# Mixer B's pair products on one stationary operand, compressed values in eight row tiles, and w_out prepared a tile earlier in a hybrid decoder layer

## The chip, the cores and the metric

The kernel runs on one core of one Trainium2 chip. The metric is the device time of one execution in microseconds (us), as the median of several runs; a profiled execution gives the trace. TensorE multiplies, VectorE (DVE) and ScalarE (ACT) do the elementwise work, GpSimd (POOL) a little, and SyncE (SP) issues the transfers. The trace shows TensorE's weight loads as an engine of their own, PEld, beside its matmuls, PE.

## The reference, cut to what matters

One decoder layer on 512 tokens of width 1024. Two mixers read one input projection, are gated, merged and put through one output projection, and a layer norm with a residual ends it.

```python
def layer(x):
    h = x @ w_in + b_in                       # 1024 -> 5912 columns
    o_a = nsa_attention(...) * silu(z_a)      # 8 heads: compressed, selected, window branches
    o_b = hgrn2(q_b, f_b, i_b, lb)            # 4 heads of 128 x 128 state
    o_b = rms_norm(o_b) * norm_g * silu(z_b)
    y = sigmoid(gm_a) * (o_a @ w_branch_a) + sigmoid(gm_b) * (o_b @ w_branch_b)
    return layer_norm(alpha * x + y @ w_out, ln_g, ln_b)

# the compressed branch: 31 blocks, per head a softmax over them
pc = masked_softmax(q @ kc.T * scale, cmp_end <= t)
o_cmp = pc @ vc                               # vc: 31 x 64 for each of two groups of four heads

# mixer B, in chunks of 64 tokens: b is the running sum of log-forget-gates within a chunk
qe = qf * exp(b); ke = k * exp(-b)
attn = where(causal, qe @ ke.T, 0)            # 64 x 64 for each chunk
o = attn @ v + qe @ state                     # and the state is carried from chunk to chunk
```

## The kernel before

Everything is laid out with channels on the 128 partitions and the 512 tokens along the free axis. Projections keep full accuracy by splitting each operand into a rounded high part and the rest (`split2`: a cast on ScalarE at line 147, a subtraction on VectorE at line 148) and multiplying three of the four combinations, so that one 128-column tile of a projection is 24 matmuls of 512 columns (`proj`). Products that are not split are issued in full precision; the trace shows each as two TensorE instructions.

TensorE's instructions are kept in the order of the code, and so are the transfers on SP. The other engines' instructions are placed by a scheduler that runs over the finished program. What TensorE does between projection matmuls is set by `_Weave`: every stage beside the projections is a generator, `weave.tick()` is called every second of the eight steps of a projection (after six matmuls), and each generator says in how many ticks it wants to go on. The table `D` holds these numbers.

Stages that matter here. `hgrn(h)` is mixer B for one of four heads. It works on pairs of 64-token chunks, 128 tokens to a pair: `e1` is the key times a decay, `qeM` the query times its decay, `at` the masked products of a pair, and the pair products are issued at lines 403 to 408. `cmp_kv` makes compressed keys `kcB` and values `vcB`, `cmp_scores` and `cmp_probs` make the softmax over blocks, and `attn_values` (line 683) multiplies probabilities and compressed values into `asum` before it goes through the selected and window branches; `attn_scores` makes the scores of these in six units. Products of part of the array stand for 32 or 64 partitions of an operand or a result.

After the projections come eight tiles of branch weights (`BRANCH`, line 873), each two groups of 12 matmuls, merged on VectorE (lines 892 and 896) into `y`. The output projection needs w_out with its column mean taken out and split: `load_out` loads 128 rows, `minus_mean` sums them on ScalarE (line 859), and `split_out` writes high and low parts (lines 868 and 869). In the branch loop, tile n loads w_out's tile n and sums and splits tile n-2; the last two are split behind the loop. Then four token tiles of 48 matmuls each form the output (line 918), with the layer norm on VectorE and the stores.

Buffers: a pool `t2` of 67 tiles of 128x512, shown as `t` in the trace, and four PSUM pools of two banks each: `pa` (projections), `pss` (scores and small products), `pst` (transposes, and the first output tile), `pso` (accumulated results). `wraw`, `whi`, `wlo` are a weight tile as loaded and its two parts.

Of the kernel before, what the change touches and what calls it, by code (L numbers as in the profile page):

```python
# [18 lines left out]
P = 128  # L19
# [3 lines left out]
EPS = 1e-5  # L23

# [22 lines left out]
def _columns(name):  # L47

    c = np.arange(_COLS[name], _COLS[name] + 128)
    if name[0] == "q" and name[1] != "b" or name[:2] == "za":  # L50
# [17 lines left out]
         r0=5, p0=4, p1=11, p2=2, b0=1, a0=1, a1=1, a2=1, a3=1, a4=2, a5=1, s0=17, s2=0, s3=1)  # L68
# [27 lines left out]
def layer_kernel(ctx: ExitStack, tc: tile.TileContext, xT, xn, w0, wi, wf, wv, small, brow, consts,  # L96
# [145 lines left out]
    vcB = cst.tile([P, 4, 128], F32, name="vcB")  # L242
    G.memset(vcB, 0.0)
# [120 lines left out]
    def hgrn(h):  # L364
# [3 lines left out]
        bc, kc, qc = chunks(b), chunks(k), chunks(qs[h])  # L368
# [9 lines left out]
        yield D["h2"]  # L378
        A.activation(e2, e2, AF.Exp)
        A.activation(e1, e1, AF.Exp)  # L380
        A.activation(eb, b, AF.Exp)
        ke = T2(256)
        kev = ke.rearrange("p (t s) -> p t s", s=64)
        A.activation(kev, bc[:, :, 0], AF.Exp, scale=-1.0)
# [5 lines left out]
        qeM, qeo = T2(), T2(256)  # L390
        ebc, qmc = chunks(eb), chunks(qeM)
        qov = qeo.rearrange("p (t s) -> p t s", s=64)
# [3 lines left out]
        V.tensor_tensor(qmc[:, :, 1], qov, ebc[:, :, 0, 63:64].to_broadcast([P, 4, 64]), ALU.mult)  # L396
# [13 lines left out]
        for v in range(2):  # L410
            V.copy_predicated(chunks(at[0:64])[:, v:4:2, 0],
                              tri[0:64, 0:64].unsqueeze(1).to_broadcast([64, 2, 64]),
                              chunks(pst_[64 * v:64 * v + 64])[:, v:4:2, 0])
        V.copy_predicated(chunks(at)[:, :, 1], tri[:, 64:128].unsqueeze(1).to_broadcast([P, 4, 64]),
                          chunks(pst_)[:, :, 1])
# [23 lines left out]
        A.activation(sq, po, AF.Square)  # L439
        A.copy(o, po)  # L440
# [55 lines left out]
    mvs, ready, vcp = [None, None], set(), []  # L496

    def cmp_kv():
# [30 lines left out]
        for g in range(2):  # L529
            for m in range(4):  # L530
                r = 32 * (2 * (m % 2) + g)
                dst, src = vcB[r:r + 32, m, 64 * g:64 * g + 64], ps[r:r + 32, 64 + 64 * g:128 + 64 * g]
                if m % 2:
                    V.tensor_copy(dst, src)
                else:
                    A.copy(dst, src)
        ready.add("cmp")
        yield 2
        vcp.extend((T2(dt=F32R), T2(dt=F32R)))
        split2(vcB.rearrange("p m d -> p (m d)"), *vcp)  # L540
# [52 lines left out]
    def cmp_scores():  # L593
# [12 lines left out]
        ss = T2(), T2()  # L606
        s6 = [s.rearrange("p (i m g n) -> p g i m n", i=4, m=2, g=2) for s in ss]
        for g in range(2):
            ps = transpose4(sT[g])
            p4 = ps.rearrange("p (i c m n) -> p c i m n", i=4, c=2, m=2)  # L610
            for c in range(2):
                V.tensor_tensor(s6[c][:, g], p4[:, c], cmask.unsqueeze(2).to_broadcast([P, 4, 2, 32]), ALU.add)
            yield 1
        for c in range(2):
            weave.start(cmp_probs(c, ss[c]), 2 * c)

    def cmp_probs(c, s):
        s3 = s.rearrange("p (x n) -> p x n", n=32)
        mx = SM(16, "mx")
# [8 lines left out]
        for m in range(2):  # L628
            mxm = mx.rearrange("p (i m g) -> p i m g", i=4, m=2)[:, :, m]
            V.tensor_tensor(mxm, mxm, gv.rearrange("p i (g m) b -> p i g m b", g=2)[:, :, :, 2 * c + m, 0], ALU.mult)  # L630
# [3 lines left out]
        PTc[c] = T2(dt=F32R), T2(dt=F32R)  # L634
        split2(ps, *PTc[c])
# [47 lines left out]
    def attn_values():  # L683
# [3 lines left out]
        yield D["b0"]  # L687
        for m in range(4):
            po = PO()
            hi, lo = (t[:, 128 * m:128 * m + 128] for t in vcp)  # L690
            T.matmul(po, hi, PTc[m // 2][0], start=True, stop=False)
            T.matmul(po, hi, PTc[m // 2][1], start=False, stop=False)
            T.matmul(po, lo, PTc[m // 2][0], start=False, stop=True)
            A.copy(asum[:, m], po)
            yield 1
# [139 lines left out]
    gm = {}  # L835
    for i in range(8):
        for c in "ab":
            name = "g%s%d" % (c, i)
            ps, m = proj(name)
            gm[name] = T2()  # L840
            with tc.issue_after(exps[-1]):
                A.activation(gm[name], ps, AF.Tanh, bias=hbias[:, m:m + 1], scale=0.5)


    wo, woraw = [], {}
    lg, lbn = [T2(), T2()], [T2(), T2()]

    def load_out(kt):
        if kt < 8:
# [183 lines left out]
```

## Time and profile before

| | |
|---|---|
| median of 3 runs | 438.39 us (437.7 to 438.88) |
| the profiled execution, its own time | 437.94 us |
| its span, first to last instruction | 436.1 us |
| TensorE busy | 428.6 us, 98% |
| VectorE busy | 304.3 us, 70% |
| ScalarE busy | 245.2 us, 56% |
| mean granted TensorE clock | 0.996 of 2.4 GHz |
| memory traffic | 41.93 MB read, 2.10 MB written |

A page of the profile gives busy time by engine, the chain of work that ended last (followed back from the last instruction to what released it), and groups of equal instructions. The trace also answers with timelines: instructions of one engine in order, equal ones merged, with the idle time before a row and what ended it in brackets. Ends of matmuls are modelled and overlap the next one's start, so the distance between starts is what an instruction costs.

### The profile page before, as it was taken

To read this page: it belongs to the slowest core of one execution; us is meant where nothing else is said; L and a number is where in the kernel's file an instruction comes from. 1 tells how busy PE (TensorE), PEld (TensorE's weight loads), DVE (VectorE), ACT (ScalarE), POOL (GpSimd) and SP (SyncE) were. 2 spreads that over 40 slices of the span, in tenths; PEclk is the share of its full clock that TensorE was granted. 3 is DMA by queue.
4 is the path that set the end of the run, shared out by engine and by line. 5 is a ranking of instruction groups with operands and counts; after the bars stand their busy time and mean duration, and the time that the engine had idled before them with its cause. 6 is when DMAs were issued, how large, how long until landed. Compare 5 with 4: busy or idle time off the path is not lost.

```text
span 436.1 us, 6086 instructions
## 1 busy us (share of the span) xinstructions
PE 428.6 (98%) x2185; PEld 359.6 (82%) x2185; DVE 304.3 (70%) x629; ACT 245.2 (56%) x490; POOL 16.3 (4%) x27
## 2 busy tenths in 40 slices
PE   9999999999999999999999999999999999999994
PEld 8888888888898878888888888888888888877884
DVE  5915669986887577976665666578755768875395
ACT  4434624613447553768866666688864646569300
POOL 2000000000010220000000010001001100000000
PEclk9999999999999999999999999999999999999998
DMA  8995400352330554132112211111212462153022
GB/s 270 396 357 173 176 0 1 86 145 74 114 95 0 170 155 157 51 116 78 48 48 59 87 51 48 50 48 48 99 48 98 167 220 87 57 157 134 1 102 92
DMA packets 20879, 47.57 MB, mean 109 GB/s; under 512 B 2929, under 2 KB 4593, under 8 KB 20849
## 3 DMA queue, kind: packets, MB, share of 16 engines
q1 hardware_dynamic: 20560, 46.92, 32.1%
q8 instruction: 17, 0.28, 0.3%
q10 hardware_dynamic: 288, 0.26, 0.2%
q14 instruction: 14, 0.11, 0.1%
HBM read 41.93 MB, written 2.10 MB: 101 GB/s over the span
## 4 chain that ended last, share of the span: by engine, by line
PE 93%; DVE 5%; ACT 1%; issue 0%; DVEq 0%; ACTq 0%
PE pa L104 59%; PE pss L104 15%; PE pso L104 12%; PE pst L108 5%; PE pst L104 2%; DVE t L869 1%; DVE t L892 1%; DVE t L148 1%; ACT t L147 1%; DVE t L896 1%; DVE wlo L148 0%; DVE t L950 0%; DVEq L1029 0%; DVE sm_nm L861 0%; DVE sm_bst L938 0%
## 5 line engine op out<-in xcount | busy, mean ns | idle before, releaser
L104 PE MATMUL pa<-t,whi 128*128 128x512 f32 x640 | 201.6, 396 | 0.0
L104 PEld LDWEIGHTS pa<-t,whi 128*128 128x128 f32 x640 | 117.0, 188 | 24.5 <-issue 1.2
L104 PE MATMUL pa<-t,wlo 128*128 128x512 f32 x320 | 125.1, 391 | 0.0
L104 PEld LDWEIGHTS pa<-t,wlo 128*128 128x128 f32 x320 | 60.1, 188 | 13.1
L147 ACT CAST whi<-wraw 128x1024 fp32r<-128x1024 f32 x46 | 48.2, 1047 | 33.7 <-PE pa L104 20.1
L148 DVE TENSOR_TENSOR wlo<-wraw,whi 128x1024 fp32r<-128x1024 f32 x46 | 57.8, 1261 | 12.0 <-ACT whi L147 11.8
L664 DVE CUSTOM_DVE_ANT_0 t<-pss,t 128x512 f32<-128x512 f32 (+3 forms) x64 | 30.1, 488 | 24.0 <-PE pss L104 24.0
L148 DVE TENSOR_TENSOR t<-pst,t 128x512 fp32r<-128x512 f32 x42 | 28.9, 690 | 17.3 <-ACT t L147 17.2
L667 ACT ACTIVATE t<-t,sm_mn 128x512 f32<-128x512 f32 (+3 forms) x64 | 35.8, 560 | 9.1 <-DVE sm_mn L664 7.4
L104 PE MATMUL pso<-t,t 128*128 128x512 f32 (+2 forms) x170 | 36.9, 352 | 0.0
L104 PE MATMUL pa<-t,t 128*128 128x512 f32 (+1 forms) x168 | 36.7, 375 | 0.0
L104 PE MATMUL pss<-t,t 128*128 128x512 f32 (+4 forms) x238 | 36.1, 307 | 0.0
L147 ACT CAST t<-pst 128x512 fp32r<-128x512 f32 x42 | 24.3, 579 | 20.4 <-PE pst L108 20.3
L104 PEld LDWEIGHTS pa<-t,t 128*128 128x128 f32 x168 | 30.3, 188 | 5.6
L104 PEld LDWEIGHTS pss<-t,t 128*128 128x128 f32 (+1 forms) x238 | 29.3, 176 | 3.7 <-DMA wraw<-in_wf_dram 0.4
L104 PEld LDWEIGHTS pso<-t,t 128*128 128x128 f32 x170 | 28.2, 196 | 4.2
L108 PE MATMUL pst<-con,t 128*128 128x128 f32 x189 | 28.6, 272 | 0.0
L108 PEld LDWEIGHTS pst<-con,t 128*128 128x128 f32 x189 | 23.2, 141 | 4.2 <-DVE t L148 0.2
L148 DVE TENSOR_TENSOR t<-t,t 128x512 fp32r<-128x512 f32 (+1 forms) x22 | 14.2, 666 | 13.5 <-ACT t L147 13.4
L104 PE MATMUL pso<-t,vv 128*128 128x512 f32 x80 | 23.1, 410 | 0.0
L147 ACT CAST t<-t 128x512 fp32r<-128x512 f32 (+1 forms) x22 | 12.7, 603 | 12.9 <-DVE t L896 12.7
L104 PE MATMUL pss<-t,whi 128*128 128x512 f32 x64 | 19.7, 389 | 0.0
(164 smaller groups left out, 532.5 us busy)
## 6 DMA issues: line engine op xcount, KB each, us to landing
wraw<-in_wf_dram SPq DMA_DIRECT2D x38, 512.0 KB, 3.6
wraw<-in_wbr_dram SPq DMA_DIRECT2D x8, 512.0 KB, 3.5
t<-in_wout_dram SPq DMA_DIRECT2D x16, 256.0 KB, 3.8
t<-in_w_dram SPq DMA_DIRECT2D x15, 256.0 KB, 5.5
t<-t SPq DMA_DIRECT2D x48, 64.0 KB, 2.0
t<-in_wi_dram SPq DMA_DIRECT2D x8, 256.0 KB, 6.1
t<-in_xn_dram SPq DMA_DIRECT2D x8, 256.0 KB, 7.1
out_dram<-t SPq DMA_DIRECT2D x8, 256.0 KB, 2.1
```

The source lines that it names most:

```text
L104: return tc.keep_in_program_order(nc.tensor.matmul(*a, **k))
L108: return tc.keep_in_program_order(nc.tensor.transpose(*a, **k))
L147: A.copy(dst_hi, src)
L148: V.tensor_tensor(dst_lo, src, dst_hi.bitcast(F32), ALU.subtract)
L664: V.tensor_tensor_reduce(out=p[:, c], in0=ps[:, c], in1=amask[:, 512 - n:512], op0=ALU.add, op1=ALU.min, scale=-0.125, scalar=3.0e38, accu ...
L667: A.activation(p[:, c], p[:, c], AF.Exp, bias=mn[:, k], scale=-1.0, accum_out=den[:, k])
L869: V.scalar_tensor_tensor(lo, raw, nm, hi.bitcast(F32), ALU.add, ALU.subtract)
L892: V.scalar_tensor_tensor(r, gm["g%s%d" % (mix, m)], 1.0, ps, ALU.add, ALU.mult)
L896: V.tensor_tensor(r, r, rb[m], ALU.add)
```

## The change

Three edits, and what follows from them in the code around.

1. `hgrn`: the pair products of a pair of chunks use the one stationary operand `e1` for both chunks. The first chunk's queries get the decay relative to the chunk's end in exchange (`qp`, an exponential with opposite sign of the same `e1`), and are scaled by 2**-64 (`FIRST`) so that the larger range fits; the first chunk's part of `o` is scaled back as it leaves PSUM. One product of 128 columns per pair stands for what were half a product of 128 columns and one of 64.
2. The compressed values: probabilities are ordered so that the four heads of a group stand in four strips of 32 partitions, and each head is one full-precision product of 32 rows by 64 columns. The zero-padded, split `vcB` and the split of the probabilities go; the four results are held in two `pso` and two `pst` banks at once.
3. w_out: `load_out`, the sum (`mean_out`) and the split are steps of `out_ahead`, which is also called behind the gate projections, so each step stands earlier. In branch iteration n it loads tile n+3, splits tile n+1 and sums tile n+2.

`attn_scores` starts a tick later (`s0` 18 for 17).

```diff
+AHEAD = 1
+FIRST = 2.0 ** -64
-         ... s0=17, s2=0, s3=1)
+         ... s0=18, s2=0, s3=1)
...
+        qp = T2()
+        qpc = chunks(qp)
         A.activation(e2, e2, AF.Exp)
+        A.activation(qpc[:, :, 0], chunks(e1)[:, :, 0], AF.Exp, scale=-1.0)
         A.activation(e1, e1, AF.Exp)
         A.activation(eb, b, AF.Exp)
-        A.activation(kev, bc[:, :, 0], AF.Exp, scale=-1.0)
...
-        V.tensor_tensor(qov, qc[:, :, 1], ebc[:, :, 1], ALU.mult)
-        V.tensor_tensor(kev, kev, kc[:, :, 0], ALU.mult)
-        V.tensor_tensor(qmc[:, :, 0], qc[:, :, 0], ebc[:, :, 0], ALU.mult)
+        V.tensor_tensor(qpc[:, :, 1], qc[:, :, 1], ebc[:, :, 1], ALU.mult)
+        V.scalar_tensor_tensor(qpc[:, :, 0], qc[:, :, 0], FIRST, qpc[:, :, 0], ALU.mult, ALU.mult)
+        V.scalar_tensor_tensor(qmc[:, :, 0], qc[:, :, 0], FIRST, ebc[:, :, 0], ALU.mult, ALU.mult)
...
-        for u in range(2):
-            T.matmul(chunks(pst_)[:, 2 * u:2 * u + 2, 0], ke[:, 128 * u:128 * u + 128],
-                     qmc[:, 2 * u:2 * u + 2, 0], start=True, stop=True)
         for t in range(4):
-            T.matmul(pst_[:, 128 * t + 64:128 * t + 128], e1[:, 128 * t:128 * t + 128],
-                     qeo[:, 64 * t:64 * t + 64], start=True, stop=True)
+            c = slice(128 * t, 128 * t + 128)
+            T.matmul(pst_[:, c], e1[:, c], qp[:, c], start=True, stop=True)
...
+        V.copy_predicated(at.rearrange("p (t s) -> p t s", s=128), tri.unsqueeze(1).to_broadcast([P, 4, 128]),
+                          pst_.rearrange("p (t s) -> p t s", s=128))
...
-        A.activation(sq, po, AF.Square)
-        A.copy(o, po)
+        A.activation(chunks(o)[:, :, 0], chunks(po)[:, :, 0], AF.Identity, scale=1.0 / FIRST)
+        A.copy(chunks(o)[:, :, 1], chunks(po)[:, :, 1])
+        A.activation(sq, o, AF.Square)
...
-        PTc[c] = T2(dt=F32R), T2(dt=F32R)
-        split2(ps, *PTc[c])
+        PTc[g] = T2()
+        A.copy(PTc[g], ps)
...
+        pc = [PO(), PO(), PT(), PT()]
+        for g in range(2):
+            for m in range(4):
+                rows = slice(32 * m, 32 * m + 32)
+                T.matmul(pc[m][64 * g:64 * g + 64], vcB[rows, 64 * g:64 * g + 64], PTc[g][rows],
+                         start=True, stop=True)
         for m in range(4):
-            po = PO()
-            hi, lo = (t[:, 128 * m:128 * m + 128] for t in vcp)
-            T.matmul(po, hi, PTc[m // 2][0], start=True, stop=False)
-            T.matmul(po, hi, PTc[m // 2][1], start=False, stop=False)
-            T.matmul(po, lo, PTc[m // 2][0], start=False, stop=True)
-            A.copy(asum[:, m], po)
-            yield 1
+            A.copy(asum[:, m], pc[m])
+        yield 1
...
+    def out_ahead(n):
+        n += AHEAD
+        load_out(n + 2)
+        if 0 <= n < 8:
+            split_out(n)
+        if 0 <= n + 1 < 8:
+            mean_out(n + 1)
...
+            out_ahead(2 * i + "ab".index(c) - 16)
...
-        load_out(n)
...
-        if n >= 2:
-            split_out(n - 2)
-    split_out(6)
-    split_out(7)
+        out_ahead(n)
```

On TensorE, where the first head's pair products stand in the order before (`pst<-con` are transposes, `pss<-t` the pair products, `pa<-` the projection around them):

```order
L104 MATMUL pa<-t_288,whi 128x512
L104 MATMUL pa<-t_287,wlo 128x512
L108 MATMUL pst<-con,t_671 128x128 x3
L104 MATMUL pss<-t_787,t_704 128x2x64 x2
L104 MATMUL pss<-t_788,t_670 128x64 x4
L104 MATMUL pa<-t_102,whi 128x512
```

The same place after:

```order
L107 MATMUL pa<-t_288,whi 128x512
L107 MATMUL pa<-t_287,wlo 128x512
L111 MATMUL pst<-con,t_670 128x128 x3
L107 MATMUL pss<-t_700,t_669 128x128 x4
L107 MATMUL pa<-t_102,whi 128x512
```

Six products became four, all of 128 columns, at the same place between the same projection matmuls.

On TensorE, the first of the four places of the compressed values before (`kh`, `kl` are parts of the keys in the score matmuls, `t_1434` and `t_1435` the parts of the values):

```order
L104 MATMUL pa<-t_287,wlo 128x512
L104 MATMUL pss<-kh_362,t_1622 128x512
L104 MATMUL pss<-kl_364,t_1622 128x512
L104 MATMUL pso<-t_1958,t_1434 128x512
L104 MATMUL pso<-t_1959,t_1434 128x512
L104 MATMUL pso<-t_1958,t_1435 128x512
```

After, all of it in one place, two ticks behind the transposes of the second group's probabilities (`t_1726`):

```order
L111 MATMUL pst<-con,t_1726 128x128 x4
L107 MATMUL pa<-t_102,whi 128x512
L107 MATMUL pa<-t_103,whi 128x512
L107 MATMUL pa<-t_102,wlo 128x512
L107 MATMUL pa<-t_142,whi 128x512
L107 MATMUL pa<-t_143,whi 128x512
L107 MATMUL pa<-t_142,wlo 128x512
L107 MATMUL pss<-kh_360,t_1715 128x512
L107 MATMUL pss<-kl_362,t_1715 128x512
L107 MATMUL pa<-t_166,whi 128x512
L107 MATMUL pa<-t_167,whi 128x512
L107 MATMUL pa<-t_166,wlo 128x512
```

```order
L107 MATMUL pa<-t_190,wlo 128x512
L107 MATMUL pso<-t_1890,vcB 64x512 x2
L107 MATMUL pst<-t_1890,vcB 64x512 x2
L107 MATMUL pso<-t_1921,vcB 64x512 x2
L107 MATMUL pst<-t_1921,vcB 64x512 x2
```

Twelve split matmuls in four places became eight full-precision ones in one place, four for each group of heads.

On ScalarE, the end of the branch stage before (line 859 sums w_out, line 868 writes the high part of its split, a `CAST` to `t` rounds a merged tile of `y`):

```order
L147 CAST t_3831<-t_3828 128x512
L859 ACTIVATE t_3811,sm_rsum<-t_3811 128x512
L859 ACTIVATE t_3812,sm_rsum<-t_3812 128x512
L147 CAST t_3851<-t_3848 128x512
L868 ACTIVATE t_3855<-t_3707,sm_nm 128x512
L868 ACTIVATE t_3857<-t_3708,sm_nm 128x512
L868 ACTIVATE t_3868<-t_3754,sm_nm 128x512
L868 ACTIVATE t_3870<-t_3755,sm_nm 128x512
L868 ACTIVATE t_3881<-t_3811,sm_nm 128x512
L868 ACTIVATE t_3883<-t_3812,sm_nm 128x512
L144 ACT_TABLE_LOAD
```

The same place after (line 847 is the split):

```order
L150 CAST t_3802<-t_3799 128x512
L847 ACTIVATE t_3806<-t_3702,sm_nm 128x512
L847 ACTIVATE t_3808<-t_3703,sm_nm 128x512
L150 CAST t_3830<-t_3827 128x512
L150 CAST t_3850<-t_3847 128x512
L147 ACT_TABLE_LOAD
```

The last split of w_out moved from behind the rounding of the last merged tile to ahead of the last two roundings.

## Rows read from the trace of the kernel before

**Rows 1.** Page, part 1: engine, busy us, share, instructions.
```profile
PE 428.6 (98%) x2185; PEld 359.6 (82%) x2185; DVE 304.3 (70%) x629; ACT 245.2 (56%) x490; POOL 16.3 (4%) x27
```
**Rows 2.** Page, part 4: the chain that ended last, by engine.
```profile
PE 93%; DVE 5%; ACT 1%; issue 0%; DVEq 0%; ACTq 0%
```
**Rows 3.** Waits of TensorE's matmuls: us in total, times, longest.
```profile
PE pso L104 <- DVE t L159: 1.1, 1, 1.1
PE pst L104 <- DVE t L869: 0.3, 1, 0.3
```
**Rows 4.** Timeline of weight loads: start, length, what, idle before; attention stage.
```profile
304.90 0.19 PEld L104 LDWEIGHTS pss<-kh,t 128*128 128x128 f32 x1 [0.43 <-issue]
```
**Rows 5.** Timeline of weight loads, the first output tile.
```profile
384.98 6.76 PEld L104 LDWEIGHTS pst<-t,t 128*128 128x128 f32 x30
392.06 0.19 PEld L104 LDWEIGHTS pst<-t,t 128*128 128x128 f32 x1 [0.33 <-ACT t L868]
392.85 3.77 PEld L104 LDWEIGHTS pst<-t,t 128*128 128x128 f32 x17 [0.60 <-DVE t L869]
396.66 0.41 PEld L104 LDWEIGHTS pso<-t,t 128*128 128x128 f32 x2
```
**Rows 6.** Timeline of weight loads, products on part of the array (rows*columns).
```profile
136.75 0.16 PEld L104 LDWEIGHTS pss<-t,ones 128*32 128x32 f32 x8 [0.15 <-issue]
137.75 0.30 PEld L104 LDWEIGHTS pa<-t,whi 128*128 128x128 f32 x2 [0.84 <-DVE vcB L534]
...
161.11 0.17 PEld L104 LDWEIGHTS pss<-t,kcB 64*32 64x32 f32 x12 [0.35 <-issue]
161.51 0.14 PEld L104 LDWEIGHTS pss<-t,kcB 64*32 64x32 f32 x4 [0.23 <-ACT t L331]
162.49 0.30 PEld L104 LDWEIGHTS pa<-t,whi 128*128 128x128 f32 x2 [0.84 <-issue]
```
**Rows 7.** Chain that ended last, in order of time: start, us, what.
```profile
76.52 1.29 PE pss L104 x12
...
363.60 2.72 PE pa L104 x12
...
397.05 10.88 PE pso L104 x48
```
**Rows 8.** Timeline of matmuls, one pair-product group (read in two stretches).
```profile
103.36 1.45 PE L104 MATMUL pss<-t,t 128*128 128x128 f32 x12
...
103.81 1.00 PE L104 MATMUL pss<-t,t 128*128 128x64 f32 x8
104.62 0.71 PE L104 MATMUL pa<-t,whi 128*128 128x512 f32 x2
```
**Rows 9.** Timeline of matmuls, ahead of and behind the compressed scores.
```profile
160.79 0.39 PE L104 MATMUL pa<-t,wlo 128*128 128x512 f32 x1
...
163.06 0.40 PE L104 MATMUL pa<-t,wlo 128*128 128x512 f32 x1
```
**Rows 10.** Timeline of ScalarE, scores of the first unit.
```profile
191.07 0.67 ACT L828 ACTIVATE t<-pa,sml 128x512 f32<-128x512 f32 x1
...
193.15 0.72 ACT L667 ACTIVATE t<-t,sm_mn 128x512 f32<-128x512 f32 x1
...
193.87 0.58 ACT L147 CAST t<-pst 128x512 fp32r<-128x512 f32 x1
```
**Rows 11.** Timeline of ScalarE, end of the branch stage.
```profile
390.77 0.62 ACT L147 CAST t<-t 128x512 fp32r<-128x512 f32 x1 [0.94 <-DVE t L896]
391.29 3.79 ACT L868 ACTIVATE t<-t,sm_nm 128x512 fp32r<-128x512 f32 x6
```
**Rows 12.** Timeline of VectorE, end of the branch stage.
```profile
391.42 0.69 DVE L148 TENSOR_TENSOR t<-t,t 128x512 fp32r<-128x512 f32 x1 [0.74 <-ACT t L147]
392.05 4.07 DVE L869 SCALAR_TENSOR_TENSOR t<-t,sm_nm,t 128x512 fp32r<-128x512 f32 x6
```
**Rows 13.** Timeline of ScalarE, last attention unit.
```profile
331.33 0.59 ACT L147 CAST t<-pst 128x512 fp32r<-128x512 f32 x1 [1.25 <-PE pst L108]
```
**Rows 14.** Timeline of the sync queue's issues.
```profile
330.30 0.86 SPq L111 DMA_DIRECT2D t<-in_wout_dram  x2
```

More of the change, by code (lines that the diff above doesn't have):

```diff
@@ L67 @@
 D = dict(h0=8, h2=4, h3=6, h4=2, h5=8, h6=5, n0=3, n1=2, n2=10, c0=1, c1=6, c2=7, c3=7,
-         r0=5, p0=4, p1=11, p2=2, b0=1, a0=1, a1=1, a2=1, a3=1, a4=2, a5=1, s0=17, s2=0, s3=1)
+         r0=5, p0=4, p1=11, p2=2, b0=1, a0=1, a1=1, a2=1, a3=1, a4=2, a5=1, s0=18, s2=0, s3=1)
 class _Weave:
@@ L241, in layer_kernel @@
     asum = cst.tile([P, 4, 512], F32, name="asum")
-    vcB = cst.tile([P, 4, 128], F32, name="vcB")
-    G.memset(vcB, 0.0)
+    vcB = cst.tile([P, 128], F32, name="vcB")
     split(0)
@@ L367, in hgrn @@
         V.tensor_tensor_scan(b, smask, lf, 0.0, ALU.mult, ALU.add)
-        bc, kc, qc = chunks(b), chunks(k), chunks(qs[h])
+        bc, qc = chunks(b), chunks(qs[h])
         bl = bc[:, :, :, 63]
@@ L389, in hgrn @@
         V.tensor_tensor(e1, e1, k, ALU.mult)
[L390 removed]
+        qeM = T2()
         ebc, qmc = chunks(eb), chunks(qeM)
[L392 to L396 removed]
+        V.tensor_tensor(qpc[:, :, 1], qc[:, :, 1], ebc[:, :, 1], ALU.mult)
+        V.scalar_tensor_tensor(qpc[:, :, 0], qc[:, :, 0], FIRST, qpc[:, :, 0], ALU.mult, ALU.mult)
+        V.scalar_tensor_tensor(qmc[:, :, 0], qc[:, :, 0], FIRST, ebc[:, :, 0], ALU.mult, ALU.mult)
+        V.tensor_tensor(qmc[:, :, 1], qpc[:, :, 1], ebc[:, :, 0, 63:64].to_broadcast([P, 4, 64]), ALU.mult)
         yield D["h4"]
@@ L494, in cmp_hidden @@
         mvs[a] = mv
-    mvs, ready, vcp = [None, None], set(), []
+    mvs, ready = [None, None], set()
     def cmp_kv():
@@ L528, in cmp_kv @@
             V.tensor_copy(kcB[64 * g:64 * g + 64], ps[64 * g:64 * g + 64, 32 * g:32 * g + 32])
[L529 to L536, printed above, removed]
+        A.copy(vcB, ps[:, 64:192])
         ready.add("cmp")
-        yield 2
-        vcp.extend((T2(dt=F32R), T2(dt=F32R)))
-        split2(vcB.rearrange("p m d -> p (m d)"), *vcp)
     gat = cst.tile([P, 4, 24], F32, name="gat")
@@ L605, in cmp_scores, with cmp_probs @@
         yield D["p2"]
-        ss = T2(), T2()
-        s6 = [s.rearrange("p (i m g n) -> p g i m n", i=4, m=2, g=2) for s in ss]
         for g in range(2):
[L609 to L612, printed above, removed]
-            yield 1
-        for c in range(2):
-            weave.start(cmp_probs(c, ss[c]), 2 * c)
-    def cmp_probs(c, s):
+            weave.start(cmp_probs(g, sT[g]), 2 * g)
+    def cmp_probs(g, src):
+        ps = transpose4(src)
+        s = T2()
         s3 = s.rearrange("p (x n) -> p x n", n=32)
+        V.tensor_tensor(s.rearrange("p (i m n) -> p i m n", i=4, n=32),
+                        ps.rearrange("p (i m n) -> p i m n", i=4, n=32),
+                        cmask.unsqueeze(2).to_broadcast([P, 4, 4, 32]), ALU.add)
         mx = SM(16, "mx")
@@ L627, in cmp_probs @@
         V.reciprocal(mx, mx)
-        for m in range(2):
-            mxm = mx.rearrange("p (i m g) -> p i m g", i=4, m=2)[:, :, m]
-            V.tensor_tensor(mxm, mxm, gv.rearrange("p i (g m) b -> p i g m b", g=2)[:, :, :, 2 * c + m, 0], ALU.mult)
+        mxm = mx.rearrange("p (i m) -> p i m", i=4)
+        V.tensor_tensor(mxm, mxm, gv[:, :, 4 * g:4 * g + 4, 0], ALU.mult)
         V.tensor_tensor(s3, s3, mx.unsqueeze(2).to_broadcast([P, 16, 32]), ALU.mult)
@@ L832, in layer_kernel @@
         zs[name] = z
[L835 to L842, printed above, removed]
     wo, woraw = [], {}
-    lg, lbn = [T2(), T2()], [T2(), T2()]
     def load_out(kt):
-        if kt < 8:
+        if 0 <= kt < 8:
             woraw[kt] = [T2(), T2()]
@@ L862, in minus_mean, with mean_out @@
         return nm
+    wmean = {}
+    def mean_out(kt):
+        wmean[kt] = minus_mean(woraw[kt])
     def split_out(kt):
         hl = [(T2(dt=F32R), T2(dt=F32R)) for _ in range(2)]
-        nm = minus_mean(woraw[kt])
+        nm = wmean[kt]
         for raw, (hi, lo) in zip(woraw[kt], hl):
@@ L870, in split_out @@
         wo.append(hl)
+    def out_ahead(n):
[5 more added lines that the diff above has]
+            mean_out(n + 1)
+    gm = {}
+    for i in range(8):
+        for c in "ab":
+            name = "g%s%d" % (c, i)
+            ps, m = proj(name)
+            gm[name] = T2()
+            with tc.issue_after(exps[-1]):
+                A.activation(gm[name], ps, AF.Tanh, bias=hbias[:, m:m + 1], scale=0.5)
+            out_ahead(2 * i + "ab".index(c) - 16)
     y, rb = [], {}
+    lg, lbn = [T2(), T2()], [T2(), T2()]
     for n, (mix, m0) in enumerate(BRANCH):
```

9 lines of the change are left out of this document (removed).

## The prediction

> **What bounds the kernel now.** I read the page's busy shares first: TensorE is busy 98% of the span, ScalarE 56% [rows 1]. A busy TensorE can still hide waiting, so the second view is the chain of work that ended last: 93% of it is TensorE [rows 2]. The third is who TensorE waited for: two entries, 1.1 us before its first instruction and 0.3 us late in the program [rows 3]. Since TensorE loads its weights ahead, I also looked at gaps in front of weight loads, which is where a late operand shows. Behind the start there are few: one of 0.43 us in the attention stage [rows 4], two around 392 us [rows 5], and some beside matmuls on part of the array [rows 6]. So nearly every microsecond is set by how many TensorE instructions there are and how far apart they start. Dense 512-column matmuls with rounded operands take 2.72 us per 12, 0.227 us each [rows 7]; that is the rate for everything that is neither short nor on part of the array. VectorE and ScalarE matter only where TensorE has to wait for them.
>
> TensorE issues in the order of the code, and the listing differs in three respects only: the four pair-product groups, the compressed-value products, and a stretch between the first score matmuls and some 18 ticks later in which score matmuls stand a tick later (a tick is six projection matmuls). Behind that the sequences are the same.
>
> **The change part by part.**
>
> *Pair products.* Before, each head issues two products of 128 columns and four of 64. A full-precision product is two TensorE instructions in the trace, so that is 12 per head; the group takes 1.29 us in the chain, for each of the four heads [rows 7]. After, four products of 128 columns are 8 instructions. The streamed columns are 512 both times, so if columns set the time nothing would be gained; that is one bound. Against it stand the rows of one group: the four 128-column instructions start 0.1125 us apart (103.36 to 103.81 us), the eight of 64 columns 0.101 us (to 104.62) [rows 8]. Half the columns save a tenth; the count sets the time. Eight at 0.1125 us are 0.90 us, eight at the whole group's mean (1.29 / 12) 0.86 us. Gain 0.39 to 0.43 us per head, 1.56 to 1.72 in all; I take **1.6 us**. VectorE and ScalarE keep as many instructions of the same sizes per head, and three masked copies become one. The new operand is written before the previous head's masked copy, and no pair group has a gap in front of its loads now, so I charge nothing; if that cover failed, the price would be some tenths per head.
>
> *Compressed values.* Removed are 12 dense matmuls of 512 columns: 12 x 0.227 = 2.72 us. They stand in four groups of three between projection matmuls, so all of it comes off TensorE's time. Added are eight full-precision products, 16 instructions, each on 32 rows and 64 columns of the array. No such shape is in the trace. The nearest row is the compressed scores: also eight products, 16 instructions, 512 columns, on 64 rows and 32 columns, from 161.11 to 162.49 us, 1.38 us, of which a 0.23 us gap is a wait for ScalarE [rows 6]. The next is the norm's sums, four products on 128 rows and 32 columns, from 136.75 to 137.75 us, 1.00 us [rows 6]. In both, 0.84 us follow the last weight load until the next, and that is about one product's two passes of 512 columns. So the tiles run beside each other, and a group costs one pair of passes plus the loads in front. Leaving and re-entering the full array costs about 0.2 us more: the matmul ahead takes 0.32 us in place of 0.23, the two behind 0.285 each [rows 6, 9]. The least is then 1.0 + 0.2 = 1.2 us; the most, short of the rivals below, is the scores' row with its gap and loads of twice the columns, about 2.0. I take 1.5, nearer the scores' row: gain **1.2 us**, between 0.7 and 1.5. The wait it could add: the group needs the second probability tile, which ScalarE copies out behind two evacuations and a weight cast. These took from 191.07 to 193.15 us, 2.1 us [rows 10]; with the copy, some 2.7 us. From that tile's transposes to the group are 14 dense matmuls, 3.2 us. So nothing, with little to spare. Two of its results sit in banks that the next transposes need, but those come seven ticks later.
>
> *w_out one tile ahead.* The first output tile's 48 products run from 384.98 us to the next tile's first load at 396.66, 11.68 us [rows 5]; the second's 48 take 10.88 [rows 7]. The difference, **0.80 us**, lies in two gaps in front of weight loads that wait for w_out's splits (ScalarE line 868, VectorE line 869) [rows 5]. ScalarE shows why: its last six splits start at 391.29, behind the rounding of the last merged tile at 390.77, which had waited for VectorE [rows 11]. After, no split stands behind that rounding. Next in line is that tile itself: VectorE starts its second part at 391.42 and is free at 392.05 [rows 12], and the 43rd product, which first needs the tile, is due at 384.98 + 42 x 0.227 = 394.5. That leaves 2.4 us, so the gain counts in full. The work is paid earlier: sums and splits of the first tiles move between the last attention roundings, where ScalarE has gaps such as 1.25 us [rows 13], and the sync queue can issue the loads long before, as it does now: at 330.30 us it is past the first pair that the code calls for with the first branch tile [rows 14]. The alternation of one w_out tile and one branch weight on that queue stays, three branch tiles earlier, with branch weights loaded three tiles ahead, so a buffer that comes free late has that cover. If all cover failed, the old 0.8 us would be paid again.
>
> Nothing else touches the path; the tail behind the last matmul is unchanged. **The sum**: 1.6 + 1.2 + 0.8 = 3.6 us. The profiled execution took 437.94 us around a span of 436.1, so 434.3 by its own time. It lies 0.45 us under the median of 438.39 of the runs shown, so I give 434.8 us for the median. With all lower ends (1.56 + 0.7 + 0.6) the gain is 2.9 us, with all upper (1.72 + 1.5 + 0.9) 4.1: 434.3 to 435.5 us, and some 0.4 us more either way for the spread of such medians.
>
> **The rivals.**
>
> *Column halves in turn.* The last four tiles share their row strips with the first four. If they had to wait until the first four are through, the group would take two pairs of passes, 2 x 0.84, plus 0.2 and a start, 2.1 us: gain 0.6 in place of 1.2, total 435.4 us. Against it: the norm's four products all use the same rows, and their eight loads came within 0.16 us [rows 6]. The Trainium skill ("TensorE: Matmul & The Clock Gate", section "The mechanism") has the rule that would do this: a weight load overlaps running matmuls only where the row group differs (elsewhere it adds: or where it goes to the background buffer). The norm's row disagrees with the strict form. Chance 0.08.
>
> *One tile after another* (the slower side). If tiles on 32 rows did not overlap at all, 16 passes of 0.42 us and the switch are 6.9 us against 2.72 removed: 4.2 lost, 2.4 gained elsewhere, 440.2 us. It decides from a group of 5.1 us on. The scores' row, 16 passes in 1.38 us [rows 6], speaks against it; for it only that no four row strips at once are in the trace. Chance 0.05.
>
> *A new TensorE wait in the attention stage.* One tick less lies between the scores of the first two units and the transposes that read them; ScalarE gets its four evacuations in a row (0.58 us each by the copies' kind [rows 10], 2.3 us) ahead of exponentials; the second probability copy has little to spare. One slip costs 0.2 to 0.5 us like the gap there now [rows 4], repeated ones up to 3 us: 435.0 to 437.8. Against it: VectorE gives up several subtractions there, and the transposes still stand four ticks, some 7 us, behind their scores. Chance 0.14, of which 0.06 costs over 2.3 us.
>
> *The w_out wait comes back as another.* If the last merged tile is now what the output waits for, the 0.8 us stay: 435.6 us. It has 2.4 us to spare [rows 5, 12]. Chance 0.05.
>
> **How the numbers follow.** Forecast 434.8 us with 0.68. A measurement of this kernel can tell about 0.3%, 1.3 us, from no change, so faster means under 437.1: forecast 0.68, column halves 0.08, the returned wait 0.05 and the smaller new waits 0.08 give 0.89. Within 0.3%: the larger new waits, 0.06. Slower: 0.05. For 8 in 10 I take 433.7 to 436.2 us: the forecast with its bounds, the column halves, the returned wait, and single slips.
>
> **What would show it.** The pair groups should be 8 instructions in about 0.88 us; the compressed values 16 instructions with about 1.3 us to the next full-array load; the first output tile 10.9 us for its 48 products, with no gap at lines that split w_out; TensorE's waits otherwise as before. A compressed group over 2.7 us, or weight-load gaps of over half a microsecond between 190 and 230 us, would make the prediction wrong.

## The result, and the profile after

| | before | after |
|---|---|---|
| median of six runs each | 438.65 us (437.7 to 439.35) | 434.30 us (433.26 to 435.3) |
| ratio | | 0.9909, 95% interval 0.9892 to 0.9926 |
| the profiled execution, its own time | 437.94 us | 433.26 us |
| its span | 436.1 us | 431.4 us |

By the medians the change makes the kernel 4.35 us faster, by the ratio 4.0 us (3.2 to 4.7). The forecast was 434.8 us, between 433.7 and 436.2. The page of after opens with its span and busy times:

```profile
span 431.4 us, 6047 instructions
PE 424.1 (98%) x2173; PEld 355.3 (82%) x2173; DVE 298.6 (69%) x610; ACT 244.6 (57%) x490; POOL 16.0 (4%) x26
```

TensorE's list of waits in after (what waited for what, us in total, times, longest) has one entry left:

```profile
PE pso L107 <- DVE t L162: 1.1, 1, 1.1
```

TensorE is as full as before [rows 1]: 4.5 us less of busy time, a span 4.7 us shorter. The 0.3 us in front of w_out's splits [rows 3] is gone. The places of the three parts follow. First, TensorE's timeline at the first head's pair products (start, length, operation, count; an end is modelled and overlaps the next start):

```profile
75.57 0.49 PE L111 MATMUL pst<-con,t 128*128 128x128 f32 x3
75.90 1.06 PE L107 MATMUL pss<-t,t 128*128 128x128 f32 x8
76.71 0.71 PE L107 MATMUL pa<-t,whi 128*128 128x512 f32 x2
```

Eight instructions, 0.81 us to the next matmul, against 1.26 for twelve [rows 8]. Next, the weight loads of the compressed values, then their matmuls:

```profile
192.43 0.14 PEld L107 LDWEIGHTS pso<-t,vcB 32*64 32x64 f32 x2 [0.35 <-ACT t L650]
...
192.52 0.14 PEld L107 LDWEIGHTS pst<-t,vcB 32*64 32x64 f32 x2
193.47 0.30 PEld L107 LDWEIGHTS pa<-t,whi 128*128 128x128 f32 x2 [0.81 <-issue]
```

```profile
192.43 0.64 PE L107 MATMUL pso<-t,vcB 32*64 32x512 f32 x2
192.44 0.65 PE L107 MATMUL pst<-t,vcB 32*64 32x512 f32 x2
192.45 0.65 PE L107 MATMUL pso<-t,vcB 32*64 32x512 f32 x2
192.47 0.64 PE L107 MATMUL pst<-t,vcB 32*64 32x512 f32 x2
192.91 0.59 PE L107 MATMUL pso<-t,vcB 32*64 32x512 f32 x2
...
193.47 0.73 PE L107 MATMUL pa<-t,whi 128*128 128x512 f32 x2
```

All sixteen loads start within 0.1 us, eight passes start within 0.05 us, the other eight 0.48 us later. Eight tiles work at once, column halves on the same rows included, and the group takes 1.04 us. Last, the loads of the output stage, one gapless row of 48, 10.88 us to the next tile where it was 11.68 [rows 5]:

```profile
381.11 10.84 PEld L107 LDWEIGHTS pst<-t,t 128*128 128x128 f32 x48
391.99 5.17 PEld L107 LDWEIGHTS pso<-t,t 128*128 128x128 f32 x23
```

Measured between the same instructions in both traces, the 4.7 us of span are these:

| stretch, to the start of the instruction named | before | after | difference |
|---|---|---|---|
| start, to the end of the first twelve `pss` products | 8.16 | 7.62 | -0.54 |
| to the next `pso` transposes and sums (106.26, now 104.03): all pair products | 98.10 | 96.41 | -1.69 |
| to the compressed scores' first load | 54.85 | 54.86 | 0 |
| the compressed scores, to the next full load | 1.38 | 1.02 | -0.36 |
| to the gap at 304.90 (now 301.02): compressed values and most of the attention | 142.41 | 141.11 | -1.30 |
| to the first output product | 80.08 | 80.09 | 0 |
| the first output tile | 11.68 | 10.88 | -0.80 |
| to the end of the span | 39.44 | 39.41 | 0 |

Three of the differences are the three parts. Two, 0.54 and 0.36 us, stand where the forecast charged nothing; the experiments ask whose they are. In what follows the first time given for a kernel is its median, and its ratio is to the runs of before that were measured together with it.

### The profile page after: what moved, and what is told of

Read it like the earlier page. It is cut to its first block, busy times and chain, and to the rows that moved or that the text cites. A ratio compares the mean times of both kernels' runs of the same rounds, so it can differ in the third digit from the quotient of the medians.

```text
span 431.4 us, 6047 instructions
## 1 busy us (share of the span) xinstructions
PE 424.1 (98%) x2173; PEld 355.3 (82%) x2173; DVE 298.6 (69%) x610; ACT 244.6 (57%) x490; POOL 16.0 (4%) x26
## 4 chain that ended last, share of the span: by engine, by line
PE 98%; DVE 1%; DVEq 0%; issue 0%; ACT 0%
PE pa L107 62%; PE pss L107 17%; PE pso L107 12%; PE pst L111 5%; PE pst L107 3%; DVE t L946 0%; DVEq L1025 0%; DVE sm_bst L934 0%; DVE t L933 0%; ACT sm_rs L941 0%; DVE sm_ag L938 0%; DVE sm_rs L942 0%; DVE t L162 0%
## 5 line engine op out<-in xcount | busy, mean ns | idle before, releaser
L151 DVE TENSOR_TENSOR t<-pst,t 128x512 fp32r<-128x512 f32 x40 | 27.5, 690 | 15.8 <-ACT t L150 15.8
L107 PE MATMUL pss<-t,t 128*128 128x512 f32 (+3 forms) x222 | 34.5, 310 | 0.0
L150 ACT CAST t<-pst 128x512 fp32r<-128x512 f32 x40 | 23.2, 580 | 18.9 <-PE pst L111 18.8
L107 PE MATMUL pso<-t,t 128*128 128x512 f32 (+2 forms) x158 | 32.9, 343 | 0.0
L107 PEld LDWEIGHTS pss<-t,t 128*128 128x128 f32 (+1 forms) x222 | 27.5, 175 | 3.7 <-issue 0.7
L107 PEld LDWEIGHTS pso<-t,t 128*128 128x128 f32 x158 | 25.3, 190 | 3.8
```

The lines of the kernel that those rows point to most:

```text
L107: return tc.keep_in_program_order(nc.tensor.matmul(*a, **k))
L150: A.copy(dst_hi, src)
L151: V.tensor_tensor(dst_lo, src, dst_hi.bitcast(F32), ALU.subtract)
```

## Experiments: each part alone

**e1_pairs** is before with the edit of `hgrn` and nothing else:

```diff
...
+            c = slice(128 * t, 128 * t + 128)
+            T.matmul(pst_[:, c], e1[:, c], qp[:, c], start=True, stop=True)
...
```

> The kernel before with the first part alone: four pair products of 128 columns in place of six of 128 and 64. If the number of TensorE instructions sets the group's time, each of the four groups takes 0.84 to 0.90 us in place of 1.29 and the kernel is 1.6 to 1.8 us faster (436.9 us beside 438.6). If the streamed columns set it, the groups stay at 1.29 us and the time is the same. The start of the program, where the profile of after stands 0.46 us ahead of before, should not move with it if that lead is chance.

435.83 us beside 438.21, ratio 0.9946 (0.9933 to 0.9960): 2.4 us (1.8 to 2.9). Each group takes 0.82 us; the stretch with all pair products is 96.33 us, 1.77 less than before. The compressed scores show no wait, 0.37 us less than before, and the start is 0.34 shorter. In the profile these two make up what the gain has beyond the 1.6 to 1.8 us expected; further on, both turn out to change from one execution to the next.

**e2_values** is before with `cmp_kv`, `cmp_probs`, the eight tiles and `s0` 18:

> The kernel before with the second part alone: the compressed values in eight row tiles, and the score matmuls a tick later. My theory: the group takes 1.0 to 1.3 us with the switch of about 0.2 us, in place of 2.72, and the wait of 0.23 us for ScalarE in the compressed scores goes too if it is this part that frees ScalarE there; together 1.5 to 1.9 us faster. Rival: column halves in turn, a group of 2.1 us, 0.6 us faster. If the attention stage pays part of it back, some 0.2 us less.

436.84 us beside 438.21, ratio 0.9968 (0.9956 to 0.9981): 1.4 us (0.8 to 1.9). From the load behind the compressed scores to the gap in the attention stage it takes 141.01 us, 1.40 less than before, with that gap unchanged at 0.43. So this part is worth 1.40; the 0.10 us that after lacks is its gap of 0.53, which before's other relatives show as well (0.53 in e1_pairs and e3_wout) and a second profile of after does not (0.43 in e9_after_again). But the wait in the compressed scores did not go: it grew to 0.88 us, so the expectation failed there.

**e3_wout** is before with `out_ahead`:

> The kernel before with the third part alone: w_out's mean and split one tile ahead. My theory: the first output tile's 48 products take 10.88 us in place of 11.68, 0.80 us faster. Rival: the last merged tile, or a branch weight that comes later on the sync queue, is now what the output waits for, and 0.3 us or less is gained.

437.18 us beside 438.21, ratio 0.9981 (0.9971 to 0.9992): 0.8 us (0.4 to 1.3). Its 48 loads run from 385.42 to 396.30 us, 10.88, without a gap. The rival falls.

**e4_half_columns** keeps the changed kernel and cuts each pair product in two:

```diff
-            T.matmul(pst_[:, c], e1[:, c], qp[:, c], start=True, stop=True)
+            for k in range(2):
+                n = slice(128 * t + 64 * k, 128 * t + 64 * k + 64)
+                T.matmul(pst_[:, n], e1[:, c], qp[:, n], start=True, stop=True)
```

> The changed kernel with each of its four pair products per head cut into two of 64 columns: 16 TensorE instructions per head in place of 8, the same 512 streamed columns and the same result. If the count sets the time: 16 x 0.101 = 1.62 us per head in place of 0.88, 2.9 us slower than after in all (437.2 us). If the streamed columns set it: the same as after (434.3 us).

437.81 us beside 438.21, ratio 0.9989 (0.9977 to 1.0001): 3.5 us more than after, by the medians and by the ratios. The weight loads of the first group, one for each instruction, and the load behind them, here:

```profile
76.03 1.86 PEld L107 LDWEIGHTS pss<-t,t 128*128 128x128 f32 x16
77.81 0.30 PEld L107 LDWEIGHTS pa<-t,whi 128*128 128x128 f32 x2
```

in after:

```profile
75.79 0.97 PEld L107 LDWEIGHTS pss<-t,t 128*128 128x128 f32 x8
76.68 0.30 PEld L107 LDWEIGHTS pa<-t,whi 128*128 128x128 f32 x2
```

and in before (the group of [rows 8]):

```profile
103.25 1.42 PEld L104 LDWEIGHTS pss<-t,t 128*128 128x128 f32 x12
104.59 0.30 PEld L104 LDWEIGHTS pa<-t,whi 128*128 128x128 f32 x2
```

1.78 us for sixteen instructions of 64 columns, 0.89 for eight of 128, 1.34 for twelve of both kinds: 0.11 us each in all three. The count sets the time, and between 64 and 128 columns the columns cost nothing of their own here. Whether the load or the matmul of an instruction sets the 0.11 us is not shown, since each instruction has one of both. Halving the columns and doubling the count gives back twice what the first part gained.

**e8_split_in_step** sets `AHEAD = 0`: tile n is split in branch iteration n.

> The changed kernel with w_out's splits in step with the branch tiles in place of one ahead: the last tile's split, two ScalarE instructions of 0.6 us and two of VectorE of 0.7, stands behind the rounding of the last merged tile. My theory: those weights are needed 42 matmuls, 9.5 us, into the output stage, and they are ready about then, so 0 to 0.3 us slower than after, the first output tile 10.9 to 11.2 us. Rival: everything behind the rounding is paid, 0.8 us slower (11.7 us for the first output tile).

434.28 us, level with after; ratio to before 0.9905 (0.9888 to 0.9922). The first output tile still takes 10.88 us. VectorE ends the last split behind the last merged tile's rounding:

```profile
390.28 0.69 DVE L151 TENSOR_TENSOR t<-t,t 128x512 fp32r<-128x512 f32 x1 [0.74 <-ACT t L150]
390.90 1.41 DVE L848 SCALAR_TENSOR_TENSOR t<-t,sm_nm,t 128x512 fp32r<-128x512 f32 x2
```

It is through at 392.31 us, and the 43rd product is due at 382.84 + 42 x 0.227 = 392.4. What pays is that no more than one tile's split stands behind the last rounding; the tile ahead is reserve.

**e11_scores_earlier** sets `s0=17` in the changed kernel.

> The changed kernel with the score matmuls of the attention units a tick earlier again, as in the kernel before (the one number of the change that I charged nothing). If the tick hides nothing and costs nothing, level with after within 0.3 us. If the later start is what keeps ScalarE's evacuations of the compressed values out of the way of the score rows, gaps of 0.2 to 0.5 us appear in front of weight loads behind 190 us, up to 1 us slower.

435.00 us beside 434.50 of after, measured together; ratio to before 0.9908 (0.9891 to 0.9925), so the runs alone do not settle it. The trace shows one longer wait, on VectorE's split of the probabilities, where after's kernels have 0.43 to 0.53 us:

```profile
302.19 0.19 PEld L107 LDWEIGHTS pss<-kl,t 128*128 128x128 f32 x1
303.17 0.42 PEld L111 LDWEIGHTS pst<-con,t 128*128 128x128 f32 x4 [0.79 <-DVE t L151]
```

From the end of the compressed scores to the first output product it takes 221.60 us, after and its repetition 221.20 and 221.14. The later tick saves 0.4 us in that trace, at another place and against another engine than I had expected.

## Experiments: tiles that share rows

**e5_one_strip** lets all eight products read the first strip of rows:

```diff
-                rows = slice(32 * m, 32 * m + 32)
+                rows = slice(0, 32)
```

> The changed kernel with all eight compressed-value products reading rows 0 to 31 (it leaves out the other three strips of rows, so it sums the wrong values): the same 16 instructions and columns, but only two different tiles of the array in place of eight. If what counts is that each tile is its own, the four products of one tile go in turn and the two tiles side by side: 8 passes of 0.43 us, a group of some 3.5 us in place of 1.04, 2.5 us slower than after (436.8 us). If a row strip serves one product at a time, 16 passes in turn: 6.9 us, 5.8 us slower (440.1 us). If the number of instructions sets it, nothing changes (434.3 us).

440.13 us; ratio to before 1.0067 (1.0043 to 1.0090). By the time alone this is the middle theory's 440.1, a strip that serves one product at a time. TensorE's rows say otherwise (in the code, column half 0 writes `pso`, `pso`, `pst`, `pst`, then half 1 the same):

```profile
193.56 1.93 PE L107 MATMUL pso<-t,vcB 32*64 32x512 f32 x4
195.33 0.59 PE L107 MATMUL pst<-t,vcB 32*64 32x512 f32 x1
195.34 0.64 PE L107 MATMUL pso<-t,vcB 32*64 32x512 f32 x1
195.76 0.59 PE L107 MATMUL pst<-t,vcB 32*64 32x512 f32 x1
195.81 0.59 PE L107 MATMUL pso<-t,vcB 32*64 32x512 f32 x1
...
197.10 1.95 PE L107 MATMUL pst<-t,vcB 32*64 32x512 f32 x4
198.98 1.22 PE L107 MATMUL pa<-t,whi 128*128 128x512 f32 x2
```

One tile takes a pass every 0.43 us. From 195.34 us on, half 1's first passes run beside half 0's last four, on the same rows. The group takes 5.42 us, twelve passes in a line and not sixteen. The rest of the 440.13 us is the clock. Two stretches of e5_one_strip (from and to, length, busy time and count of TensorE, its loads, VectorE, ScalarE and GpSimd, granted clock, DMA share, GB/s):

```profile
190.00:193.00 3.00, 3.00 (x16) 2.52 (x15) 2.52 (x5) 2.75 (x6) 0.00 (x0) 1.00 0.10 27
199.00:202.00 3.00, 3.00 (x8) 2.42 (x8) 0.00 (x0) 0.59 (x1) 0.00 (x0) 0.50 0.00 0
```

Behind 5.4 us with one or two tiles of 32x64 at work the granted clock stood at 0.50, its lower level of 1.2 GHz, and eight matmuls fill 3 us where some 13 would. From the group's end to the gap in the attention stage it takes 108.94 us, in after 107.55, so the clock costs some 1.4 us in this execution. The agreement of the total with a wrong theory was chance: 4.4 us of group and 1.4 of clock. Nine executions took 439.85 to 443.68 us, the four above 442 at a mean granted clock of 0.985 to 0.988 where the others have 0.991 to 0.995, so the price of the clock seems to vary.

**e12_halves_in_turn** is the same with the two loops exchanged, so that the column halves alternate in the code.

> As e5_one_strip (all products read rows 0 to 31 and so leave out three strips), but the two column halves by turns in the code: half 0, half 1, half 0, and so on. In e5_one_strip the group took 5.42 us: a pass of one tile every 0.43 us, and the second half's first pass started beside the fifth of the first half, not at the end of its eight. If the halves of one strip run side by side as soon as they are next in the order: 8 passes of 0.43 us and the end, a group of 3.5 to 4.0 us, 2.4 to 3.0 us slower than after, and more if the granted clock falls behind it again (to 0.50 from 199 to 202 us in e5_one_strip). If a row strip served one product at a time: 16 passes, 6.9 us.

436.89 us, 2.4 above after's 434.50, measured together; ratio to before 0.9971 (0.9950 to 0.9993). The group:

```profile
193.49 1.93 PE L107 MATMUL pso<-t,vcB 32*64 32x512 f32 x8
195.25 1.88 PE L107 MATMUL pst<-t,vcB 32*64 32x512 f32 x8
197.06 0.72 PE L107 MATMUL pa<-t,whi 128*128 128x512 f32 x2
```

Sixteen passes in 3.57 us, two abreast, and in this execution the granted clock stays at 1.00 from 198 to 204 us. (One of the eight executions took 440.18 us at a mean granted clock of 0.989, so it may have fallen there; no profile shows that one.) So column halves of one strip run side by side; the prediction's first two rivals are excluded, not only unlikely. e5_one_strip is slower because of the order in the code: half 1 started early, but by three passes only.

## Experiments: the wait nobody changed

The compressed scores wait for ScalarE's evacuation of the fourth query tile [rows 6]. ScalarE waits for VectorE, and VectorE runs beside GpSimd's four multiplications by mixer B's norm factors (line 466 after, 469 before), the last of which starts, in every profile that has it on GpSimd, when its factors land by DMA.

**e6_no_mult** is before without these multiplications:

```diff
-            G.tensor_tensor(o, o, rms[h], ALU.mult)
```

> The kernel before without the four multiplications by the norm factors on GpSimd (they are left out, so mixer B's output is not normalised). In the traces the compressed scores wait 0 to 0.88 us for ScalarE, which waits for VectorE, and VectorE's subtraction of 1024 columns takes 1.22 us alone but up to 1.87 where one of these multiplications runs. My theory: GpSimd's multiplication beside it slows VectorE, so without it the subtraction takes 1.22 us, the gap in the compressed scores (0.23 us in before) is gone, the group takes 1.02 us in place of 1.38, and the kernel is 0.3 to 0.4 us faster than before. Rival: the wait is made by the order on VectorE and ScalarE, and stays.

437.60 us beside 438.27, ratio 0.9980 (0.9968 to 0.9993): 0.7 us (0.3 to 1.4), more than the 0.36 us that the profiles show. The wait is gone and the group takes 1.02 us. VectorE's subtraction ahead of it, in before:

```profile
155.28 1.70 DVE L148 TENSOR_TENSOR wlo<-wraw,whi 128x1024 fp32r<-128x1024 f32 x1 [2.08 <-ACT whi L147]
```

and in e6_no_mult:

```profile
155.75 1.22 DVE L148 TENSOR_TENSOR wlo<-wraw,whi 128x1024 fp32r<-128x1024 f32 x1 [2.81 <-ACT whi L147]
```

In before GpSimd's third multiplication had started at 154.60 us, for 1.29 us, and the subtraction took 1.70 in place of 1.22.

**e9_after_again** is the changed kernel unedited, for a second profile.

> The changed kernel once more, unedited, for a second profile and as the measure for the two kernels beside it. If the 0.46 us at the start and the 0.36 us in the compressed scores, by which the profiled execution of after stood ahead beyond the three parts, are chance of the execution, they come out anew here: a start of 6.6 to 7.8 us to the end of the first twelve pss products, a gap of 0 to 0.88 us in the compressed scores, median 434.0 to 434.8 us. If they belong to the change, both are as in after.

434.50 us beside 438.86, ratio 0.9902 (0.9886 to 0.9919). Both unexplained gains are absent from its profile: its start ends at 8.23 us, later than the 6.6 to 7.8 expected and close to before's 8.16, and the compressed scores wait 0.88 us:

```profile
159.42 0.17 PEld L107 LDWEIGHTS pss<-t,kcB 64*32 64x32 f32 x12 [0.35 <-issue]
160.47 0.14 PEld L107 LDWEIGHTS pss<-t,kcB 64*32 64x32 f32 x4 [0.88 <-ACT t L333]
```

The reason for the wait stands in two rows, the fourth multiplication on GpSimd and the step of the scores' chain on VectorE that falls beside it. VectorE and GpSimd in after:

```profile
156.09 0.69 DVE L570 TENSOR_TENSOR t<-t,t 128x512 f32<-128x512 f32 x1
```

```profile
156.45 1.47 POOL L466 TENSOR_TENSOR t<-t,t 128x512 f32<-128x512 f32 x1 [4.66 <-DMA t<-t]
```

and in e9_after_again:

```profile
156.62 1.79 DVE L570 TENSOR_TENSOR t<-t,t 128x512 f32<-128x512 f32 x1
```

```profile
156.04 1.82 POOL L466 TENSOR_TENSOR t<-t,t 128x512 f32<-128x512 f32 x1 [4.43 <-DMA t<-t]
```

Where VectorE's instruction starts first, it takes 0.69 us, and GpSimd's some longer than its usual 1.29. Where GpSimd's starts first, by 0.16 to 0.62 us in six profiles, VectorE's takes 1.78 or 1.79, and TensorE pays 0.87 or 0.88. A few tenths between the two starts decide, and GpSimd's hangs on the landing of a transfer. The Trainium skill ("GPSIMD Engine Reference", section "1. Specifications") says that GpSimd shares its SBUF interfaces with VectorE and contends with VectorE instructions that have two SBUF inputs; this one has two, and the trace agrees with 0.69 against 1.79 us.

Six profiles share after's code up to here: one shows no wait, five 0.87 or 0.88 (e5, e8, e9, e11, e12). Of before's code there are two, with 0.23 and 0.40 (e3). So the 0.36 us gained in after's profile is chance, and in most profiles after loses about half a microsecond here against before.

**e7_vector_mult** puts the four multiplications on VectorE in the changed kernel (`V.tensor_tensor`).

> The changed kernel with the four multiplications by the norm factors on VectorE in place of GpSimd. If GpSimd's operations beside VectorE cost more than 0.6 us of VectorE each, this is level with or up to 0.3 us faster than after (434.0 to 434.3 us). If VectorE now waits for the factors in its order, the compressed scores wait again: up to 0.9 us slower.

433.82 us beside 438.27, ratio 0.9895 (0.9877 to 0.9914), a little under the 434.0 to 434.3 expected. The third one, 0.69 us, now stands in VectorE's own order ahead of the scores' chain, and a wait of 0.36 us is left.

**e10_third_on_gpsimd** leaves that one on GpSimd, where it runs ahead of the scores' chain:

```diff
-            G.tensor_tensor(o, o, rms[h], ALU.mult)
+            (G if h == 2 else V).tensor_tensor(o, o, rms[h], ALU.mult)
```

> The changed kernel with three of the four multiplications by the norm factors on VectorE and the third left on GpSimd, where VectorE is idle. My theory: no GpSimd operation runs beside VectorE's work for the compressed scores and none stands in its way, so the group takes 1.02 us in every execution: 0.2 to 0.6 us faster than the mean execution of after (433.6 to 434.1 us). Rival: the wait is worth nothing in most executions, level with after.

433.42 us (433.04 to 434.00) beside 434.50 for after, measured together (433.80 to 435.21), ratio to before 0.9881 (0.9863 to 0.9898): the lowest median of the study, 1.1 us below after's. Against e7_vector_mult (433.34 to 434.20) the difference is not clear. Its compressed scores:

```profile
159.11 0.18 PEld L107 LDWEIGHTS pss<-t,kcB 64*32 64x32 f32 x16 [0.35 <-issue]
160.13 0.30 PEld L107 LDWEIGHTS pa<-t,whi 128*128 128x128 f32 x2 [0.84 <-issue]
```

No wait, 1.02 us. The spans of the two profiles differ by 1.3 us: 1.01 here, 0.27 at the start.

**The start** needed no kernel of its own. The first twelve projection products in after:

```profile
4.29 1.90 PE L107 MATMUL pso<-t,t 128*128 128x256 f32 x12
```

and in e9_after_again, the same code:

```profile
4.14 2.67 PE L107 MATMUL pso<-t,t 128*128 128x256 f32 x12
```

The same instructions take 1.90 or 2.67 us, and those that began earlier ended later. Two stretches of 2 us, after first (columns as above):

```profile
4.00:6.00 2.00, 2.00 (x14) 1.85 (x14) 1.73 (x6) 0.46 (x2) 0.00 (x0) 1.00 0.83 252
4.00:6.00 2.00, 2.00 (x10) 1.93 (x10) 1.53 (x5) 0.41 (x1) 0.00 (x0) 1.00 0.87 259
```

Fourteen matmuls against ten at a printed clock of 1.00. But that 1.00 is not a reading: the trace's clock records begin only at 4.55 us in after and at 6.20 us in e9_after_again, and a view prints 1.00 for the time ahead of them. TensorE has been at work since 1.05 us in both. Where nothing else holds them up, its products of 256 columns start 0.21 us apart until about the first record and 0.12 us apart behind it. 0.21 us for 256 columns is the pace of the lower level, 1.2 GHz: at a recorded 0.50, e5_one_strip's matmuls of 512 columns start about 0.43 us apart.

So the start is a matter of when the clock rises, and the same code had it at 4.55 and at 6.20 us. All fourteen profiles fit: six with the first record before 4.6 us take 1.90 to 1.93 us for the twelve products, the others, from 5.24 to 7.14 us, 2.24 to 3.12. The ten profiles with the pair part have it at 3.94 to 6.66 us, the four without at 5.98 to 7.14. Since one code spans much of that, chance can explain after's lead of 0.54 us; that the pair part has no share in it is not shown.

## Why the prediction was right, point by point

**Pair products: right, with one misread row.** Forecast 1.6 us (1.56 to 1.72), measured 1.69, and 1.77 alone. I had read 0.1125 against 0.101 us [rows 8] as a tenth saved by half the columns. The weight loads show no such saving: 0.11 us each for either kind. So the eight instructions cost 0.89 us, as I had said (0.86 to 0.90), but the twelve before cost 1.34 and not the 1.29 that I took from the chain, and four times 0.45 is 1.8.

**Compressed values: mechanism right, size at the edge.** Forecast 1.2 us, between 0.7 and 1.5; measured 1.40. I had taken the group with its switch at 1.5 us, nearer to the compressed scores' row [rows 6]. It took 1.04 us and all in all 2.72 - 1.40 = 1.32, near the bound's lower end of 1.2, because all sixteen loads start within 0.1 us. The gap in front of it is 0.35 us, as in front of the compressed scores, so the second probability tile was not late.

**w_out: right to the hundredth.** Forecast 0.80, measured 0.80 in after and e3_wout. The spare time of the last merged tile was less than I said, 1.3 us and not 2.4: VectorE is through with it at 389.29 us, and the 43rd product is due at 381.11 + 42 x 0.227 = 390.6.

**The new wait: not where I looked.** I gave 0.14 to a new TensorE wait in the attention stage behind 190 us. There is no evidence for it: the 0.1 us by which after's one gap is longer is absent from its second profile. The wait that most profiles of after do show is ahead of it, in the compressed scores, 0.88 us for ScalarE, VectorE and GpSimd. I read the 0.23 us there [rows 6] as a fixed cost of that group. I had not asked why ScalarE was late, and so missed that it depends on a transfer and moves when anything ahead moves.

**The sum** was 3.6 us. The three parts measure 1.69 + 1.40 + 0.80 = 3.9, so they carry the forecast. Between the profiles the account closes: e9_after_again's execution, 434.73 us, is 3.2 below before's 437.94, and that is the three parts less the 0.65 us by which its wait in the compressed scores is longer. The medians differ by more, 4.35 us, or 4.0 by the ratio. Before's profiled execution is quicker than most, 0.3 to 0.9 us under the medians of before's runs (438.21 to 438.86), so up to 1 us of the measured gain lies in executions of before that no profile shows, and its cause is open. So the median agrees with the forecast partly by luck: the longer wait and this gain, neither of which the forecast held, went opposite ways.

## What to carry to other kernels

On a kernel whose TensorE is full, count its instructions by kind and spacing: small full-precision products cost by their number, so one of 128 columns beats two of 64, and eight products on 32 rows and 64 columns took 1.04 us together where all eight tiles differ, against 3.57 us on two tiles. Give a group of such products every strip and column half before it comes back to the first, since passes of one tile followed each other at 0.43 us here. And ask of each short wait on the critical engine which transfer or which engine beside it sets it; one profile shows one draw of it.

## What the runs showed of the hardware

- Passes on different tiles do not start in the order of the code alone: in e5_one_strip half 1's first pass started at 195.34 us, while three passes of half 0 that stand ahead of it still had to start (195.76 to 196.62). The Trainium skill ("TensorE: Matmul & The Clock Gate", section "The mechanism") has matmuls start and end strictly in the program's order; where the starts above differ from that, the measurement decides. Its rule that a weight load overlaps running matmuls only where the row group differs does not fit in its strict form either: both column halves loaded and ran on one row group. Its other form, a load into the background buffer, is not excluded.
- Full-precision instructions with a stationary operand of 128x128 started their weight loads 0.11 us apart, with 64 columns to stream as with 128 (e4_half_columns, after).
- In the profiled executions the granted clock fell to 0.50 for 3 us behind 5.4 us of one or two tiles at work (e5_one_strip), and did not behind 3.6 us of two (e12_halves_in_turn) or 1.04 us of eight (after).
- The clock's rise at the start moved between executions: the first record of 1.00 stands at 3.94 to 7.14 us in fourteen profiles, and products of 256 columns started 0.21 us apart ahead of it and 0.12 us behind it.
- A VectorE instruction of 0.69 us took 1.78 or 1.79 where a GpSimd multiplication had started 0.16 to 0.62 us ahead of it (six profiles).
